# Hymba trunk step: background pieces issued ahead of the newest unit's sigmoids and scans in the prompt attention loop

## The chip, the cores and the metric

The kernel is one program on one core of a Trainium2 chip. The metric is the device time of one execution in microseconds (us). The core's engines each work through a queue of their own, in the order in which the program issued the instructions: PE (TensorE: matmuls, and transposes done as matmuls; PEld is its weight load), DVE (VectorE), ACT (ScalarE), POOL (GpSimd), and SP (SyncE), which here only issues DMAs. PE writes its results to PSUM; DVE and ACT copy them from there.

## The reference, cut to what matters

One layer of a hybrid decoder runs over a prompt (4096 tokens, width 1024) and a sample batch (8 sequences of 4 tokens). Four branches (a state space model, a short convolution, a stick-breaking attention and a cross-attention to 256 memory tokens) read one input projection; each branch is normalized and gated, and an output projection and a last norm follow. The change concerns the prompt's stick-breaking attention, 4 heads of 64 channels:

```python
z = jnp.einsum("nqhd,nkhd->nhqk", q.astype(f32), k.astype(f32)) * (HEAD_DIM ** -0.5)
z = z + bias.astype(f32)[None, :, None, None]
mask = k_pos[None, :] < q_pos[:, None]
log_beta = jax.nn.log_sigmoid(z)
log_1m = jnp.where(mask, jax.nn.log_sigmoid(-z), 0.0)
rev = lax.cumsum(log_1m, axis=3, reverse=True)
excl = jnp.concatenate([rev[..., 1:], jnp.zeros_like(rev[..., :1])], axis=-1)
wts = jnp.where(mask, jnp.exp(log_beta + excl), 0.0)
return jnp.einsum("nhqk,nkhd->nqhd", wts, v.astype(f32)).astype(q.dtype)
```

A weight is sigmoid(z) of its key times the product of sigmoid(-z) over all later keys up to the query. The kernel forms the product as a running product from right to left (a scan on DVE) instead of a sum of logarithms.

## The kernel before, in words

The program has three stretches. Up to about 1970 us it projects the prompt, runs the sample's attention and the other branches. From about 1975 to 3345 us runs the prompt's attention, the subject here. The rest is the tail: the last output tiles.

**Units.** The attention is cut into 72 blocks (query chunk `qc` of 512 tokens, head pair `hp`, key block `kb` of 512 keys from the diagonal back to 0), and each block into four units `qt` of 128 queries: 288 units, numbered 0 to 287. In the text "unit 159" is the 160th; it is also the number of the pass of the loop that begins it. A unit has two heads. On the diagonal (`kb == qc`) it has 128 to 512 keys, elsewhere 512.

**What a pass issues.** The loop at the end of `hymba_kernel` (L1874 to L1898) issues in pass i, in this order:
- `scores` of unit i (L1439): 6 matmuls on PE into two PSUM tiles `z`. There are four such tiles, so the scores of unit i+2 need both heads of unit i to be read to the end.
- in odd passes `out_step` (L1604): one or two pieces of the output projection, 6 matmuls each (L1560 to L1562), which add up to an output tile; DVE adds the residual (`yb<-wo,xt`), and now and then a tile's input is prepared (`mt<-mr`, on ACT and DVE).
- `stage_b` of unit i-3 (L1481): the weights are transposed on PE, head 0 into one PSUM tile `wt`, head 1 into another (L1487), and copied to SBUF (`wT<-wt`), head 1 by ACT, head 0 by DVE, one time in four by ACT. The tag `wt` has two buffers, and almost every matmul of the background writes into the same tag.
- `weights` of unit i (L1456): for each head ACT makes two sigmoids (`om<-z`, `bt<-z`), DVE the scan (L1470, `T<-om,cy,z`; it names `z` as a second operand, so `z` comes free with its end), POOL the product `bt<-bt,T` and a carry `cy` (L1475) for the next key block.
- `run_bg` (L105): each background generator is run to its next `yield`. The sample's generator `smp` is left out before pass 10 and in all odd passes.
- in odd passes `stage_c` (L1493): matmuls of two units' weights with V (`ya<-wT,vt`); at the end of a query chunk's head pair ACT copies and squares `ya`.

**Background generators.** `wout_gen` (L1415): 8 pieces in passes 5 to 12, each loads 128 rows of the output weights and splits them on ACT and DVE (`wo<-stg`). `sample_gen` (L1630): the sample's branches, about a hundred small pieces in even passes to pass 220. `merge_c` (L1520): once for each query chunk, in four pieces: sums of squares on PE (L1525), their copy on ACT (`ev<-so`) and a product with the gate, which is loaded in the same piece (L1531); a matmul (L1535) and `rr` (L1538); nothing; and a transpose (L1544, `bc`) with two products `Yc<-Yc,bc` on DVE. `out_norm` (L1570): for each output tile a square on ACT (`xt<-yb`, with a read of its accumulator), a small DVE step (L1574), a power on POOL, in a following pass a product on DVE (L1577), then the store.

The names at the changed place: `z` in the loop holds the scores of unit i, `sa[i]` its weights, `bg` the list of generators.

Of the kernel before, what the change touches and what calls it, by code (L numbers as in the profile page):

```python
# [29 lines left out]
def hymba_kernel(ctx: ExitStack, tc: tile.TileContext, x_p, x_s, cache_k, cache_v, s_re, s_im, s_conv,  # L30
# [10 lines left out]
    def act(out, in_, f=AF.Copy, **kw):  # L41
        return S.activation(out, in_, f, **kw)  # L42

    def tt(eng, out, a, b, op):
        return eng.tensor_tensor(out=out, in0=a, in1=b, op=op)  # L45
# [59 lines left out]
    def run_bg(skip=None):  # L105
        for g in list(bg):
            if g is not skip and next(g, "end") == "end":
                bg.remove(g)
# [1008 lines left out]
    def load_q(qc, hp):  # L1117
        t = x_tile("qst", F32R).rearrange("p (l n) -> p l n", l=2)
        SP.dma_start(t.bitcast(F32), qscr[:, hp * 128:(hp + 1) * 128, qc * 512:(qc + 1) * 512].rearrange("l p n -> p l n"))
        qst_t[qc, hp] = t  # L1120
# [186 lines left out]
    i = 0  # L1307
# [96 lines left out]
    def load_kv(*b):  # L1404
        load_keys(*b, sb.tile([128, 2, 512], F32R, tag="kst", name="kst", bufs=2))
        load_v2(*b)
# [32 lines left out]
    def scores(qc, hp, kb, qt):  # L1439
        ks = kst_t[qc, hp, kb]  # L1440
        diag = kb == qc
        n = (qt + 1) * 128 if diag else 512

        qs = qst_t[qc, hp]
        zs = [ztile() for h in range(2)]
        for lq_, lk in ((0, 0), (0, 1), (1, 0)):
            for h in range(2):
                r = slice(64 * h, 64 * h + 64)
                mm(zs[h][:, 0:n], qs[r, lq_, qt * 128:(qt + 1) * 128], ks[r, lk, 0:n],  # L1449
                   start=(lq_ + lk == 0), stop=(lq_ == 1 and not diag))  # L1450
        if diag:
            for h in range(2):
                mm(zs[h][:, n - 128:n], idr, maskr, start=False, stop=True)  # L1453
        return zs, n

    def weights(zs, n, qc, hp, kb, qt):  # L1456
        diag = kb == qc
        ws = []
        for h in range(2):
            z, hd = zs[h], 2 * hp + h  # L1460
            om = om2[h]
            T = sb.tile([128, 513], F32, tag="T2", name="T2", bufs=4)
            c = cy[:, 2 * qt + h:2 * qt + h + 1]
            bt = sb.tile([128, 512], F32, tag="bt2", name="bt2", bufs=7)
            act(om[:, 0:n], z[:, 0:n], AF.Sigmoid, scale=-0.125, bias=nb4[:, hd:hd + 1])
            act(bt[:, 0:n], z[:, 0:n], AF.Sigmoid, scale=0.125, bias=b4[:, hd:hd + 1])
            if n < 512:
                V.memset(om[:, n:n + 1], 1.0)

            V.tensor_tensor_scan(T[:, 0:n + 1][:, ::-1], om[:, 0:n + 1][:, ::-1],  # L1470
                                 z[:, 0:1].to_broadcast([128, n + 1]), 1.0 if diag else c,
                                 op0=ALU.mult, op1=ALU.bypass)
            tt(P, bt[:, 0:n], bt[:, 0:n], T[:, 1:n + 1], ALU.mult)
            if kb:
                P.tensor_copy(c, T[:, 0:1])  # L1475
            ws.append(bt)
        return ws, n
# [3 lines left out]
    def stage_b(qt, ws, n):  # L1481

        for h in range(2):
            t = wtp()
            cnt[0] += 1
            for k in range(n // 128):
                tr(t[:, k, :], ws[h][:, k * 128:(k + 1) * 128], ident)  # L1487
            if qt % 2 == 0:
                wts[h] = sb.tile([128, 4, 2, 128], F32, tag="wT2", name="wT2", bufs=4)
            (act if h or cnt[0] % 8 == 1 else V.tensor_copy)(wts[h][:, 0:n // 128, qt % 2, :], t[:, 0:n // 128, :])  # L1490
        return dict(wts)
# [376 lines left out]
    units = [(qc, hp, kb, qt) for (qc, hp, kb) in blocks for qt in range(4)]  # L1868
# [3 lines left out]
    sa, sbq = {}, {}  # L1872
    LAG = 3
    for i in range(nu + LAG + 1):  # L1874
        j = i - LAG
        z = None
        if i < nu:
            qc, hp, kb, qt = units[i]
            if qt == 0:
                bi = i // 4  # L1880
                if bi + 1 < len(blocks):
                    load_kv(*blocks[bi + 1])
                    if blocks[bi + 1][:2] != (qc, hp):
                        load_q(*blocks[bi + 1][:2])
            z = scores(*units[i])
            if i % 2:
                out_step(max(0.0, 8.0 * (4 * NCH - 5) - ost["done"]) * 2 / (nu - i + 1))

        if 0 <= j < nu:
            ws, n = sa.pop(j)  # L1890
            sbq[j] = stage_b(units[j][3], ws, n)
        if z is not None:
            sa[i] = weights(*z, *units[i])
        if i == 5:
            bg.append(wout_gen())
        run_bg(smp if i < 10 or i % 2 else None)
        if j >= 2 and j % 2 == 0:
            stage_c(*units[j - 1], sbq[j - 1])  # L1898
    ost["tail"] = True
# [43 lines left out]
```

## Time and profile before

| | |
|---|---|
| median of 3 runs | 3415.83 us (3399.83 to 3421.22) |
| profiled execution | 3414.53 us, its span 3412.8 us |
| mean granted TensorE clock over the span | 0.973 |
| busy share of the span | PE 93%, PEld 67%, DVE 67%, ACT 52%, POOL 37% |

A row of a group gives busy time, mean time of one instruction, and the idle time of its engine just before it with what ended that idle time. A row of the timeline gives the start, the length from the first start to the last end of what is merged in it, the engine, and in brackets the idle time before it. Waits on several semaphores are put down to the one that came last in the trace.

### The profile page before, as it was taken

How to read it: one execution, taken by the hardware profiler on the slowest of the kernel's cores; microseconds unless marked ns; L12 is line 12 of the kernel's file. 1: busy time of each engine (PE TensorE's matmuls, PEld its weight loads, DVE VectorE, ACT ScalarE, POOL GpSimd, SP SyncE). 2: the span in 40 equal slices, each digit the busy share in tenths (PEclk: the TensorE clock that was granted, in tenths of full speed). 3: DMA queues.
4: the chain of work that ended last, by engine and by line, in shares of the span. 5: the costliest groups of instructions: out<-in, count | busy, mean ns of one | idle time of the engine just before them, and what ended most of it. 6: DMA issues, size and time to landing. Idle time of an engine off the chain costs nothing. (4 is left out here: it accounts for less than half of the span.)

```text
span 3412.8 us, 65273 instructions
## 1 busy us (share of the span) xinstructions
PE 3164.8 (93%) x23383; PEld 2282.1 (67%) x23383; DVE 2283.0 (67%) x3628; ACT 1780.8 (52%) x3324; POOL 1267.6 (37%) x1721
## 2 busy tenths in 40 slices
PE   7888999999999999999999988998999888999998
PEld 6556767667677677676676655666666555666667
DVE  5875667666676676676756566667666777677773
ACT  3435544443444444444434366666656666667771
POOL 1465322222231122222222045555545445555560
PEclk9899999999999999999999979999999999999999
DMA  6677887888877878878887443232323223222223
GB/s 212 194 209 224 279 268 238 264 279 274 267 251 254 286 245 290 263 234 277 270 262 214 142 163 103 91 97 87 97 87 95 71 91 102 94 86 75 88 66 117
DMA packets 382179, 623.57 MB, mean 183 GB/s; under 512 B 54568, under 2 KB 245488, under 8 KB 381856
## 3 DMA queue, kind: packets, MB, share of 16 engines
q1 hardware_dynamic: 344912, 484.90, 45.1%
q0 software_dynamic: 36944, 134.50, 11.9%
q8 instruction: 186, 3.05, 0.4%
q14 instruction: 137, 1.12, 0.1%
HBM read 539.33 MB, written 79.95 MB: 181 GB/s over the span
## 5 line engine op out<-in xcount | busy, mean ns | idle before, releaser
L45 POOL TENSOR_TENSOR bt<-bt,T 128x512 f32<-128x512 f32 (+3 forms) x576 | 605.9, 1052 | 632.2 <-DVE T L1470 417.0
L218 PE MATMUL pj<-xh,whl 128*128 128x512 f32 (+1 forms) x1792 | 724.9, 405 | 0.0
L1470 DVE TENSOR_TENSOR_SCAN T<-om,cy,z 128x513 f32<-128x513 f32 x448 | 549.7, 1268 | 249.3 <-ACT bt L42 96.6
L220 PE MATMUL pj<-xh,whl 128*128 128x512 f32 (+1 forms) x1792 | 658.7, 368 | 9.4 <-DVE whl L45 9.4
L219 PE MATMUL pj<-xh,whl 128*128 128x512 f32 (+1 forms) x1792 | 658.2, 367 | 0.1
L888 POOL DMA_INDIRECT kt<-in_cache_sb_k_dram,idxk x256 | 298.4, 1166 | 898.5 <-DVE kT L1056 787.0
L42 ACT ACTIVATE wT<-wt 128x512 f32<-128x512 f32 (+3 forms) x360 | 194.5, 556 | 448.8 <-PE wt L1487 448.2
L218 PEld LDWEIGHTS pj<-xh,whl 128*128 128x128 f32 x1792 | 344.3, 192 | 120.2 <-issue 82.0
L220 PEld LDWEIGHTS pj<-xh,whl 128*128 128x128 f32 x1792 | 344.0, 192 | 70.3 <-DVE whl L45 12.3
L42 ACT ACTIVATE bt<-z,b 128x512 f32<-128x512 f32 (+3 forms) x576 | 385.2, 669 | 0.0
L42 ACT ACTIVATE om<-z,nb 128x512 f32<-128x512 f32 (+3 forms) x576 | 380.4, 660 | 2.8 <-PE z L1453 2.8
L219 PEld LDWEIGHTS pj<-xh,whl 128*128 128x128 f32 x1792 | 345.6, 193 | 44.9 <-issue 8.6
L1487 PE MATMUL wt<-ident,bt 128*128 128x128 f32 x2112 | 299.5, 281 | 35.2 <-DVE Yc L45 13.5
L1056 DVE STREAM_TRANSPOSE kT<-kt 128x1024 f32<-128x1024 f32 x256 | 315.3, 1232 | 14.9 <-DMA kt<-in_cache_sb_k_dram,idxk 10.3
L1449 PE MATMUL z<-kst,qst 64*128 64x512 f32 (+3 forms) x1704 | 300.1, 424 | 24.2 <-DVE T L1470 21.7
L1487 PEld LDWEIGHTS wt<-ident,bt 128*128 128x128 f32 x2112 | 241.4, 143 | 105.4 <-issue 59.0
L45 DVE TENSOR_TENSOR whl<-stg,whl 128x1024 fp32r<-128x1024 f32 x191 | 234.1, 1226 | 109.3 <-ACT whl L42 99.0
L1503 PE MATMUL ya<-wT,vt 128*64 128x256 f32 (+1 forms) x2176 | 262.8, 382 | 0.3 <-DVE wT L1490 0.3
L42 ACT ACTIVATE whl<-stg 128x1024 fp32r<-128x1024 f32 x192 | 203.1, 1058 | 85.7 <-issue 36.6
L1449 PEld LDWEIGHTS z<-kst,qst 64*128 64x128 f32 x1704 | 152.3, 191 | 129.8 <-issue 52.2
L1560 PE MATMUL wo<-wo,mt 128*128 128x512 f32 x512 | 221.4, 432 | 2.3 <-ACT mt L42 2.3
L1562 PE MATMUL wo<-wo,mt 128*128 128x512 f32 x512 | 206.5, 403 | 0.5 <-DVE mt L45 0.5
(756 smaller groups left out, 4890.5 us busy)
## 6 DMA issues: line engine op xcount, KB each, us to landing
vt<-in_cache_sb_v_dram SPq DMA_DIRECT2D x1024, 128.0 KB
stg<-in_w_in_dram SPq DMA_DIRECT2D x192, 512.0 KB
kst<-kscr SPq DMA_DIRECT2D x71, 512.0 KB
xt<-in_x_prompt_dram SPq DMA_DIRECT2D x64, 512.0 KB
pkt<-pack_d SPq DMA_DIRECT2D x64, 449.0 KB
vt<-vscr SPq DMA_DIRECT2D x71, 256.0 KB
mr<-mscr SPq DMA_DIRECT2D x32, 512.0 KB
out_dram<-yb SPq DMA_DIRECT2D x32, 512.0 KB
```

Source lines behind the costliest of these rows:

```text
L42: return S.activation(out, in_, f, **kw)
L45: return eng.tensor_tensor(out=out, in0=a, in1=b, op=op)
L218: mm(o[:, t0:t1], hi[:, k, :], xh[:, k, 0, t0:t1], start=(k == 0), stop=False)
L219: mm(o[:, t0:t1], hi[:, k, :], xh[:, k, 1, t0:t1], start=False, stop=False)
L220: mm(o[:, t0:t1], lo[:, k, :], xh[:, k, 0, t0:t1], start=False, stop=(k == KT - 1))
L888: P.indirect_dma_start(out=kq[j], out_offset=None, in_=ck_rows, in_offset=bass.IndirectOffsetOnAxis(ap=idxk[:, u // NU, gg:gg + 1], axis=0))
L1056: V.transpose(kts[j], kq.pop(j))
L1449: mm(zs[h][:, 0:n], qs[r, lq_, qt * 128:(qt + 1) * 128], ks[r, lk, 0:n], start=(lq_ + lk == 0), stop=(lq_ == 1 and not diag))
L1470: V.tensor_tensor_scan(T[:, 0:n + 1][:, ::-1], om[:, 0:n + 1][:, ::-1], z[:, 0:1].to_broadcast([128, n + 1]), 1.0 if diag else c, op0=ALU. ...
L1487: tr(t[:, k, :], ws[h][:, k * 128:(k + 1) * 128], ident)
L1503: mm(ya[0][h * 64:h * 64 + 64, q0 * 128:(qt + 1) * 128], v[:, k, h * 64:h * 64 + 64], wTs[h][:, k, q0 - qt + 1:2, :].rearrange("p a b -> p ...
L1560: mm(o, mt[:, k, 0, :], wo[:, k, 0, cs], start=(k == 0), stop=False)
```

## The change

In each pass the call of `weights` moves behind `run_bg`. Nothing else changes: the same instructions, the same buffers.

```diff
         if 0 <= j < nu:
             ws, n = sa.pop(j)
             sbq[j] = stage_b(units[j][3], ws, n)
-        if z is not None:
-            sa[i] = weights(*z, *units[i])
         if i == 5:
             bg.append(wout_gen())
         run_bg(smp if i < 10 or i % 2 else None)
+        if z is not None:
+            sa[i] = weights(*z, *units[i])
         if j >= 2 and j % 2 == 0:
             stage_c(*units[j - 1], sbq[j - 1])
```

`weights` issues nothing on PE and no DMA, so the order on PE and on SP's queue stays as it was; ACT, DVE and POOL change theirs. On DVE, at units 174 to 176, where a chunk's merge ends in an odd pass (the scans stand as SCALAR_TENSOR_TENSOR; `mt` is `out_step`'s, `Yc` the merge's, `g<-wt` the sample's). Before:

```order
L45 TENSOR_TENSOR mt<-mr,mt 128x8x128
L1470 SCALAR_TENSOR_TENSOR T_32698<-om_0_23909,cy,z 128x513
L1470 SCALAR_TENSOR_TENSOR T_32705<-om_1_23910,cy,z 128x513
L45 TENSOR_TENSOR Yc<-Yc,bc 128x512 x2
L1490 COPY wT_32689<-wt 128x4x128
L1470 SCALAR_TENSOR_TENSOR T_32753<-om_0_23909,cy,z 128x513
L1470 SCALAR_TENSOR_TENSOR T_32760<-om_1_23910,cy,z 128x513
L1793 COPY g_32772<-wt 128x512
```

With the change:

```order
L45 TENSOR_TENSOR mt<-mr,mt 128x8x128
L45 TENSOR_TENSOR Yc<-Yc,bc 128x512 x2
L1470 SCALAR_TENSOR_TENSOR T_32707<-om_0_23909,cy,z 128x513
L1470 SCALAR_TENSOR_TENSOR T_32714<-om_1_23910,cy,z 128x513
L1490 COPY wT_32689<-wt 128x4x128
L1793 COPY g_32758<-wt 128x512
L1470 SCALAR_TENSOR_TENSOR T_32760<-om_0_23909,cy,z 128x513
L1470 SCALAR_TENSOR_TENSOR T_32767<-om_1_23910,cy,z 128x513
```

The products `Yc` and the sample's copy `g<-wt`, both of which empty a `wt` buffer, now stand ahead of the scans of their pass instead of behind them.

On ACT, at unit 158, an even pass with an output tile's square. Before:

```order
L42 ACTIVATE wT_31732<-wt 128x4x128
L42 ACTIVATE om_0_23909<-z,nb_88 128x512
L42 ACTIVATE bt_31777<-z,b_87 128x512
L42 ACTIVATE om_1_23910<-z,nb_88 128x512
L42 ACTIVATE bt_31784<-z,b_87 128x512
L42 ACTIVATE xt_30818,ss_31802<-yb 128x1024
```

With the change:

```order
L42 ACTIVATE wT_31732<-wt 128x4x128
L42 ACTIVATE xt_30818,ss_31788<-yb 128x1024
L42 ACTIVATE om_0_23909<-z,nb_88 128x512
L42 ACTIVATE bt_31793<-z,b_87 128x512
L42 ACTIVATE om_1_23910<-z,nb_88 128x512
L42 ACTIVATE bt_31800<-z,b_87 128x512
```

The square of 1024 columns stands ahead of the unit's four sigmoids.

On DVE, at units 158 and 159, the same tile's steps and a sample piece of 158. Before:

```order
L1490 COPY wT_31725<-wt 128x4x128
L1470 SCALAR_TENSOR_TENSOR T_31776<-om_0_23909,cy,z 128x513
L1470 SCALAR_TENSOR_TENSOR T_31783<-om_1_23910,cy,z 128x513
L1801 COPY g_31587<-sms 128x256
L1786 COPY g_31584<-g_31581 64x4 x4
L1574 TENSOR_SCALAR ss_31802<-ss_31802 128x1
L1470 SCALAR_TENSOR_TENSOR T_31846<-om_0_23909,cy,z 128x513
L1470 SCALAR_TENSOR_TENSOR T_31853<-om_1_23910,cy,z 128x513
L1577 SCALAR_TENSOR_TENSOR yb<-yb,ss_31802,fg 128x1024
L1490 COPY wT_31837<-wt 128x4x128
```

With the change:

```order
L1490 COPY wT_31725<-wt 128x4x128
L1801 COPY g_31573<-sms 128x256
L1786 COPY g_31570<-g_31567 64x4 x4
L1574 TENSOR_SCALAR ss_31788<-ss_31788 128x1
L1470 SCALAR_TENSOR_TENSOR T_31792<-om_0_23909,cy,z 128x513
L1470 SCALAR_TENSOR_TENSOR T_31799<-om_1_23910,cy,z 128x513
L1577 SCALAR_TENSOR_TENSOR yb<-yb,ss_31788,fg 128x1024
L1470 SCALAR_TENSOR_TENSOR T_31847<-om_0_23909,cy,z 128x513
L1470 SCALAR_TENSOR_TENSOR T_31854<-om_1_23910,cy,z 128x513
L1490 COPY wT_31837<-wt 128x4x128
```

The sample's copies and L1574 stand ahead of the scans of 158, L1577 ahead of those of 159 and no longer between them and the copy `wT`.

## Rows read from the trace of the kernel before

**Rows 1.** The page's first part, busy time of each engine over the whole span, its share and its instructions.

```profile
PE 3164.8 (93%) x23383; PEld 2282.1 (67%) x23383; DVE 2283.0 (67%) x3628; ACT 1780.8 (52%) x3324; POOL 1267.6 (37%) x1721
```

**Rows 2.** Busy time by stretch (from:to, length, then us and instructions of each engine, granted clock, DMA share, GB/s): the first passes, a stretch of the middle, the last passes of the attention.

```profile
1990.00:2020.00 30.00, 23.62 (x146) 15.39 (x144) 25.49 (x37) 26.55 (x53) 20.70 (x25) 0.78 0.61 195
2400.00:2800.00 400.00, 361.05 (x2366) 251.16 (x2363) 273.66 (x371) 251.34 (x462) 201.05 (x302) 0.96 0.30 91
3200.00:3345.00 145.00, 138.50 (x878) 94.66 (x877) 101.68 (x108) 101.81 (x178) 80.30 (x119) 1.00 0.24 77
```

**Rows 3.** The waits of PE from 1975 to 3345 us: what waited, on what, us in total, times, the longest.

```profile
PE z L1449 <- DVE T L1470: 21.7, 70, 1.2
PE wt L1487 <- DVE Yc L45: 13.5, 7, 3.0
PE wt L1725 <- DVE wT L1490: 7.1, 6, 1.4
...
PE wt L1487 <- DVE g L1793: 4.3, 4, 1.6
PE wt L1487 <- POOL cy L1475: 4.1, 6, 1.4
...
PE wt L1487 <- DVE rr L1538: 3.4, 2, 1.7
...
PE wt L1487 <- DVE g L1711: 1.9, 5, 0.5
...
PE wt L1487 <- DVE g L45: 1.7, 3, 0.6
...
PE wt L1487 <- ACT ev L42: 1.2, 1, 1.2
...
PE wt L1487 <- DVE msT L1661: 1.1, 1, 1.1
```

**Rows 4.** The timeline around the end of a merge, units 174 to 176 (start, length, engine, line, operation).

```profile
2808.40 1.09 POOL L45 TENSOR_TENSOR bt<-bt,T 128x512 f32<-128x512 f32 x1
2808.50 1.02 DVE L1786 COPY g<-g 64x4 f32<-64x4 f32 x1
...
2809.63 0.17 DVE L1786 COPY g<-g 64x4 f32<-64x4 f32 x1
...
2810.38 1.23 DVE L45 TENSOR_TENSOR mt<-mr,mt 128x1024 fp32r<-128x1024 f32 x1
2810.91 0.62 PE L1544 MATMUL bc<-ident,rr 128*128 128x128 f32 x4 [0.34 <-ACT wT L42]
...
2812.49 2.45 DVE L1470 TENSOR_TENSOR_SCAN T<-om,cy,z 128x513 f32<-128x513 f32 x2 [0.89 <-issue]
...
2814.87 1.26 DVE L45 TENSOR_TENSOR Yc<-Yc,bc 128x512 f32<-128x512 f32 x2
...
2816.04 0.68 DVE L1490 COPY wT<-wt 128x512 f32<-128x512 f32 x1
...
2816.27 0.63 PE L1487 MATMUL wt<-ident,bt 128*128 128x128 f32 x4 [1.59 <-DVE Yc L45]
...
2816.78 0.66 PE L1791 MATMUL wt<-ident,g 128*128 128x128 f32 x4
```

**Rows 5.** The timeline around units 158 to 160, with an output tile's square and its product, and two sample pieces.

```profile
2727.19 1.09 ACT L42 ACTIVATE xt<-yb 128x1024 f32<-128x1024 f32 x1
2727.46 1.25 DVE L1470 TENSOR_TENSOR_SCAN T<-om,cy,z 128x513 f32<-128x513 f32 x1
...
2732.74 0.96 PE L1449 MATMUL z<-kst,qst 64*128 64x512 f32 x6
...
2732.86 2.46 DVE L1470 TENSOR_TENSOR_SCAN T<-om,cy,z 128x513 f32<-128x513 f32 x2 [2.16 <-issue]
...
2735.24 1.26 DVE L1577 SCALAR_TENSOR_TENSOR yb<-yb,ss,fg 128x1024 f32<-128x1024 f32 x1
...
2735.41 0.66 PE L1791 MATMUL wt<-ident,g 128*128 128x128 f32 x4 [0.69 <-ACT wT L42]
...
2736.00 0.97 PE L1449 MATMUL z<-kst,qst 64*128 64x512 f32 x6
...
2739.38 0.66 DVE L1793 COPY g<-wt 128x512 f32<-128x512 f32 x1
...
2740.19 0.63 PE L1487 MATMUL wt<-ident,bt 128*128 128x128 f32 x4 [1.20 <-DVE g L1793]
```

**Rows 6.** Busy time by stretch (columns as in Rows 2) of the five stretches in which the clock stood at half right behind one of the waits of Rows 3: the first, the last, and their sum.

```profile
2036.10:2042.90 6.80, 5.87 (x28) 4.40 (x30) 3.06 (x10) 2.75 (x8) 1.92 (x5) 0.50 0.80 222
...
2578.80:2582.20 3.40, 3.40 (x12) 2.27 (x9) 2.16 (x5) 1.50 (x3) 2.58 (x5) 0.50 0.94 311
sum 20.20, PE 19.27 PEld 14.21 DVE 11.39 ACT 12.35 POOL 6.77; mean PE 3.85 PEld 2.84 DVE 2.28 ACT 2.47 POOL 1.35
```

**Rows 7.** Groups of moved work on DVE from 1975 to 3345 us (line, engine, operation, tiles, count, busy us, mean ns of one, idle before).

```profile
L1531 DVE SCALAR_TENSOR_TENSOR Yc<-Yc,gnc,ev 128x512 f32<-128x512 f32 x16 | 11.8, 773 | 4.0 <-DMA ev<-gscr 4.0
L1786 DVE COPY g<-g 64x4 f32<-64x4 f32 x32 | 11.8, 369 | 0.3
...
L45 DVE TENSOR_TENSOR wo<-stg,wo 128x1024 fp32r<-128x1024 f32 x8 | 10.6, 1324 | 0.7 <-ACT wo L42 0.6
```

**Rows 8.** The same for ACT.

```profile
L42 ACT ACTIVATE xt<-yb 128x1024 f32<-128x1024 f32 x26 | 28.2, 1086 | 0.0
...
L42 ACT ACTIVATE wo<-stg 128x1024 fp32r<-128x1024 f32 x8 | 8.7, 1084 | 0.1
L42 ACT ACTIVATION_READ_ACCUMULATOR xt<-yb 128x1 f32 x26 | 5.9, 226 | 0.0
...
L42 ACT ACT_TABLE_LOAD x2 | 2.6, 1283 | 0.0
```

## The prediction, made before the changed kernel was timed

> **What bounds the kernel now.** I read the engine totals first, then the stretches, then PE's waits, then the timeline around two typical places. PE is busy for 93% of the span [rows 1], and in the middle of the attention for 361 of 400 us, against 274 of DVE and 251 of ACT [rows 2]. PE's order stays the same with the change, so the time is PE's work plus PE's idle time, and the question is which idle time goes and which comes. In the middle 39 us of 400 are idle; in the last passes, where the sample's pieces have ended, 6.5 of 145 [rows 2]. The reader should see in the list of waits that PE's idle time has two roots [rows 3]: scores that wait for the scan of two units ago (70 times, 21.7 us, 0.3 us each), and matmuls that wait for one of the two `wt` buffers. Of the latter, those on L1487 wait for a background piece to empty a buffer: 13.5 + 4.3 + 4.1 + 3.4 + 1.9 + 1.7 + 1.2 + 1.1 = 31.2 us (the 4.1 on POOL's `cy` I count with them: after a merge's L1538 that carry was long made). These are the waits that the change is aimed at. Those of background matmuls on the copy `wT`, as L1725's 7.1 us in 6 waits, hang on a copy that stands ahead of both the moved and the unmoved work.
>
> What does delay cost? That differs by the parity of the pass. Unit 158 (even): its second scan ends at 2728.71 and the scores of 160 start at 2732.74, 4.0 us later [rows 5]; in between PE has an output piece to do. Unit 159 (odd): its scans end at 2735.32 and the scores of 161 start at 2736.00, after a wait of 0.69 us in front of a sample matmul [rows 5]. So an even unit's scans can come 2 to 4 us late for nothing, an odd unit's hardly at all. But in the odd pass DVE stood idle 2.16 us before the scans, waiting for ACT's sigmoids [rows 5]: work put there is free.
>
> **The change part by part.**
>
> **End of a merge (odd pass, 8 chunks, 7 waits).** Now `Yc` follows the scans: they end at 2814.94, `Yc` at 2816.13, and the transposes of head 1 wait 1.59 us [rows 4]. With the change `Yc` starts when `mt` and `bc` are done, at about 2811.6, and ends at 2812.9, before those transposes are due at about 2814.6. Before the scans only 0.89 us were free [rows 4], so these start some 0.4 us late, at 2812.9, and end at 2815.4. What is late next: the sample's matmul L1791 waits for the copy `wT`, which follows the scans, to about 2816.1, so here 0.6 of 1.59 us is won; where no sample matmul follows, nearly all. Of 13.5 us I take 10; bounds 0 and 13.5.
>
> **Sample pieces (even pass).** A copy such as L1793 at 2739.38 makes the transposes of the next pass wait 1.20 us [rows 5]. It moves ahead of scans with 2 to 4 us to spare, and behind it PE goes on to `stage_c` and scores that need nothing late. L1793, L1711, `g` on L45, `msT` and `ev` sum to 10.2 us [rows 3]; I take 10, bounds 0 and 10.2.
>
> **The merge's `rr` (odd pass).** 3.4 + 4.1 us [rows 3]. L1538 is small and fits the idle time before the scans, but PE then runs into the same copy `wT` as above in half of the cases. I take 5, bounds 0 and 7.5.
>
> **Clock.** Behind five of these waits the trace shows the clock at 0.50, the 1.2 GHz level, for 20.2 us in all [rows 6], nearly all of it PE work, of which half is lost: 10 us. With the waits mostly gone I take 6; bounds 0 and 10.
>
> **Squares (26 in this stretch, even pass).** 1.09 + 0.23 us on ACT [rows 8] now stand ahead of the four sigmoids. Cover: the 4.0 us of unit 158. Where the following odd pass has one output piece instead of two, the cover is smaller. I take +2; bounds 0 and the whole 34 us (28.2 + 5.9). The sample copies at the same place (as L1786) add about 1 us to DVE, not to ACT, and lie in the same cover. The power on POOL goes ahead of the products; it needs only DVE's small L1574, and nobody waits for it before the next pass.
>
> **L1577 (odd pass).** 1.26 us into 2.16 us of idle time [rows 5]: 0. It no longer stands between the scans and `wT`.
>
> **A merge's first piece (8, even pass).** L1531 waits for a gate tile whose load is issued in the same piece; before, the scans covered that load and the wait was still 4.0 us in all [rows 7]. Now two scans, 2.5 us, no longer cover it, and ACT's `ev` waits for PE ahead of the sigmoids. 2.5 us each, against the cover of 2 to 4: I take +3; bounds 0 and 20.
>
> **The eight `wo` pieces (passes 5 to 12).** Here ACT is busy 26.6 of 30 us and DVE 25.5 [rows 2], and there is no output piece to make cover. 1.08 us on ACT each, then 1.32 on DVE [rows 7, 8], the second beside the first sigmoid. In a stretch that ACT fills the order matters little: +3; bounds 0 and 8.7.
>
> **The sample's softmax piece (once).** It loads a table, 1.28 us [rows 8], waits for DVE, and loads back; ahead of the sigmoids that is about 5 us against 3 of cover: +2.
>
> **Buffers.** `wt` hands out its two buffers otherwise in about ten places: seven background matmuls now wait for DVE's copy instead of ACT's, three the reverse. By 7.1 / 6 = 1.2 us [rows 3] against 0.69 [rows 5] that is 4 x 0.5: +2; bounds -2 and +5.
>
> **Pairs of DVE and POOL.** The first of four small copies L1786 takes 1.02 us, a later one 0.17, and it ends when POOL's product ends (2808.40 + 1.09) [rows 4]. So moved pieces may meet a product at their new place too. On odd passes POOL is idle there, on even ones DVE's `wT` uses up 0.68 of the 1.09 us: 0 in the sum, as it lies in the cover. The Trainium skill (SBUF — State Buffer, section "SBUF: two separate sides") says that DVE and GpSimd share one pair of ports as an exclusive lock for a whole instruction, whoever comes first, for DVE operations with two SBUF inputs too; by that rule the eight `wo` steps, each behind a product of the unit before, could lose up to a whole product each. That is rival D.
>
> **Sum.** -10 -10 -5 -6 = -31, and +2 +3 +3 +2 +2 = +12: -19 us. Against the profiled execution of 3414.5 us this gives **3395 us**. The median of the runs, 3415.8, differs by 1.3 us and changes nothing.
>
> **The rivals.**
> - **A, the wait is handed on.** The freed transposes are followed at once by scores or a sample matmul that hang on the odd scans, as at unit 175, where 0.6 of 1.59 us remain. If all places were like it, 25 becomes about 10, the clock gives nothing, and with +12 the time is about 3416. For: 70 waits of scores on scans already. Against: most sample pieces sit in even passes. It is also what happens if the freed buffer is not the one awaited.
> - **B, more falls away.** The whole 31 us, 10 from the clock, and half of the costs: 3414.5 - 41 + 6, about 3380, and lower if sample matmuls wait less for a `wT` that is no longer behind L1577. For: the covers of 2 to 4 us. Against: the loop through the odd unit is nearly closed.
> - **C, slower.** The covers are not there: a piece at the head of ACT or DVE holds up the sigmoids and scans behind it, in even passes as well. Price: squares 34.1, L1786 11.8, L1531 11.8 [rows 7, 8], together +58; with the freed waits at 16 that gives about 3456. It decides from the point where an even unit's scans end after the scores two units on are due, 4.0 us at unit 158 [rows 5]. Speaks against it: delays of 1.3 to 2.5 us are below that.
> - **D, the port.** Up to 1.1 us on each of eight `wo` steps in a stretch without cover: +9, 3404.
>
> **How the numbers follow.** The forecast (3383 to 3408) has 0.52, A 0.14, B 0.18, C 0.09, D 0.07. About 1%, 34 us, is what a measurement of this kernel can tell from no change: faster means below 3382, slower above 3450. Faster: most of B and a little of the forecast's edge, 0.23. Slower: most of C, 0.08. Within 1%: 0.69. The range reaches from B's middle with somewhat more, 3368, to A with its costs doubled, 3428; outside lie C and B's end.
>
> **What would show it.** In the trace after: PE's waits on `Yc`, `g` and `rr` gone from L1487's row (step right if 31 us fall below 8); scores' waits on scans, 21.7 us, growing by no more than 10 (if by 20, A); DVE's idle time before the scans filled, by L1577 in odd passes; the scores of an even unit + 2 still starting after its scans (if PE waits there, C); the first 30 us of the `wo` pieces no longer than 33; the granted clock at or above 0.973. I am wrong if the time comes out above 3428 with the L1487 waits gone, for then a cover that I read at one unit does not hold for the others.

## The result, and the profile after

| | before | after |
|---|---|---|
| median of 5 runs each, side by side | 3407.11 us (3399.83 to 3421.22) | 3381.80 us (3378.01 to 3391.03) |
| ratio after to before, 95% interval | | 0.9917 [0.9897, 0.9937] |
| profiled execution | 3414.53 us | 3391.03 us |
| span and mean granted clock | 3412.8 us, 0.973 | 3389.3 us, 0.974 |

The change gains 0.83%, some 28 us (21 to 35). The profiled executions differ by 23.5 us. All of it lies in the prompt's attention. At first the changed kernel falls behind: unit 4 begins 1.2 us later than before, unit 13, after the `wo` pieces, 3.5 us later. From there it gains: unit 18 begins 0.1 us earlier, unit 96 15 us, unit 240 24 us.

The totals of the page after, to be held against [rows 1]: the same instructions, PE a little shorter.

```profile
PE 3156.3 (93%) x23383; PEld 2280.9 (67%) x23383; DVE 2278.2 (67%) x3628; ACT 1780.1 (53%) x3324; POOL 1252.3 (37%) x1721
```

Busy time by stretch after (columns as in [rows 2]): passes 5 to 12, from the scores of unit 5 to those of unit 13, the middle, and the whole attention.

```profile
1986.18:2019.26 33.08, 27.18 (x159) 18.05 (x158) 24.18 (x43) 26.41 (x57) 16.32 (x26) 0.76 0.61 193
...
2400.00:2800.00 400.00, 364.39 (x2371) 255.88 (x2370) 271.63 (x381) 249.90 (x460) 198.15 (x300) 0.95 0.30 90
...
1975.00:3322.00 1347.00, 1232.30 (x7963) 851.25 (x7964) 958.24 (x1254) 902.99 (x1661) 708.52 (x1063) 0.97 0.31 96
```

The first and the last of these for the kernel before:

```profile
1984.95:2015.74 30.79, 25.62 (x159) 17.34 (x158) 24.28 (x42) 26.54 (x56) 19.11 (x24) 0.78 0.61 196
...
1975.00:3345.00 1370.00, 1237.07 (x7952) 849.23 (x7952) 961.39 (x1253) 902.16 (x1658) 723.02 (x1063) 0.96 0.30 94
```

PE's idle time in the attention is the length minus the busy time: 1370.00 - 1237.07 = 132.9 us before, 1347.00 - 1232.30 = 114.7 us after. So 18 us of the 23 are idle time; the rest is PE work that took 4.8 us less, because less of it ran at 1.2 GHz: the clock record of these two stretches has 102.0 us at 0.50 before and 92.2 after, and half of the difference is 4.9.

The waits of PE after (to be held against [rows 3]):

```profile
PE z L1449 <- DVE T L1470: 29.5, 77, 1.5
PE wt L1725 <- DVE wT L1490: 9.7, 8, 1.4
PE wt L1791 <- DVE wT L1490: 9.2, 8, 1.4
...
PE so L1525 <- DVE smr L1650: 2.1, 1, 2.1
...
PE wt L1487 <- DVE rr L1538: 0.9, 1, 0.9
PE wt L1487 <- DVE ss L1574: 0.8, 1, 0.8
PE wt L1487 <- ACT wT L42: 0.8, 1, 0.8
PE wt L1487 <- ACT ev L42: 0.7, 1, 0.7
```

`Yc`, `g` and the carry are gone from L1487's waits, and 0.9 us of `rr` is left. But two other kinds grew: scores on scans from 21.7 to 29.5 us, and background matmuls on `wT`, as L1725 from 7.1 to 9.7.

### The profile page after: what moved, and what is told of

The parts are those of the page before. It is cut to its first block, busy times and chain, and to the rows that moved or that the text cites. A ratio compares the mean times of both kernels' runs of the same rounds, so it can differ in the third digit from the quotient of the medians.

```text
span 3389.3 us, 65303 instructions
## 1 busy us (share of the span) xinstructions
PE 3156.3 (93%) x23383; PEld 2280.9 (67%) x23383; DVE 2278.2 (67%) x3628; ACT 1780.1 (53%) x3324; POOL 1252.3 (37%) x1721
## 3 DMA queue, kind: packets, MB, share of 16 engines
q0 software_dynamic: 36944, 134.50, 12.1%
## 5 line engine op out<-in xcount | busy, mean ns | idle before, releaser
L1449 PE MATMUL z<-kst,qst 64*128 64x512 f32 (+3 forms) x1704 | 302.1, 423 | 32.6 <-DVE T L1470 29.5
L1487 PE MATMUL wt<-ident,bt 128*128 128x128 f32 x2112 | 292.7, 280 | 3.3 <-DVE rr L1538 0.9
L1487 PEld LDWEIGHTS wt<-ident,bt 128*128 128x128 f32 x2112 | 242.5, 143 | 65.7 <-issue 40.8
```

## Where the time went: the accounts of all runs

A table by run. For each I summed PE's idle time between the first and the last transpose of L1487 by what the waiting matmul was (scores, L1487, everything else = background), and the time at 0.50 in the trace's clock record, from the entries that begin and end in that stretch (the one that runs across its start adds 8 to 12 us in every row). One profiled execution each, so a difference of 2 or 3 us, or of 10 us at half clock, is not to be read; even the first transpose of L1487, ahead of which the versions hardly differ, came anywhere from 1973.1 to 1983.0 us. The stretch begins and ends a little inside the one above, so the sums are slightly smaller. The ratio is that of the runs, with its 95% interval; us are (ratio - 1) x 3410.

The columns "full clock" and "clock" split the gain by the runs themselves, for each has its span and mean granted clock on record. Span times clock is the span that would be left if nothing were lost at 1.2 GHz, an estimate that takes PE to be at work there throughout ([rows 6]: 19.27 of 20.20 us); span times (1 - clock) is what the clock took. Given is the mean against the runs of the kernel before beside it, with a 95% interval (for the change, against 70 runs of the kernel before from the experiments). In these 70 the first part is 3322 to 3326 us in each of four groups and scatters by 2 to 3 us from run to run, the second is 82 to 89 us and scatters by 4 to 7: executions of one kernel differ mostly by clock.

| pieces ahead of the scans | ratio | us | full clock | clock | idle | L1487 | scores | background | at 1.2 GHz |
|---|---|---|---|---|---|---|---|---|---|
| none (before) | 1 | 0 | 0 | 0 | 132.0 | 35.2 | 24.2 | 72.6 | 85.3 |
| all (the change) | 0.9917 [0.9897, 0.9937] | -28 | -18 ±5 | -9 ±10 | 113.6 | 3.3 | 32.6 | 77.7 | 78.5 |
| in odd passes only | 0.9964 [0.9952, 0.9976] | -12 | -12 ±2 | -1 ±5 | 119.0 | 8.3 | 27.9 | 82.7 | 75.1 |
| in even passes only | 0.9924 [0.9904, 0.9945] | -26 | -14 ±3 | -10 ±8 | 121.2 | 22.5 | 29.5 | 69.2 | 75.1 |
| output norm only | 1.0008 [0.9994, 1.0022] | +3 | -2 ±2 | +4 ±5 | 130.6 | 30.9 | 24.3 | 75.4 | 105.8 |
| all but the output norm | 0.9877 [0.9859, 0.9894] | -42 | -27 ±8 | -12 ±9 | 109.2 | 3.9 | 29.9 | 75.5 | 71.7 |
| all but the squares' piece | 0.9962 [0.9944, 0.9980] | -13 | -18 ±2 | +4 ±6 | 117.1 | 4.3 | 33.0 | 79.8 | 78.5 |
| all but L1577 | 0.9889 [0.9868, 0.9910] | -38 | -30 ±5 | -11 ±8 | 108.0 | 3.9 | 29.1 | 75.0 | 58.0 |
| odd passes, no output norm | 0.9963 [0.9948, 0.9978] | -13 | -13 ±3 | 0 ±7 | 121.1 | 13.8 | 27.4 | 79.9 | 92.2 |
| even passes, no output norm | 0.9952 [0.9939, 0.9964] | -16 | -14 ±3 | -4 ±8 | 119.9 | 22.1 | 28.6 | 69.3 | 54.6 |
| all, ACT pad in even passes | 0.9999 [0.9984, 1.0013] | 0 | -9 ±2 | +8 ±6 | 118.6 | 1.7 | 40.7 | 76.2 | 88.7 |
| all, ACT pad in odd passes | 1.0207 [1.0180, 1.0235] | +71 | +40 ±3 | +27 ±16 | 161.1 | 2.9 | 79.2 | 79.0 | 119.5 |
| all but the output norm, `wT` copies exchanged | 0.9719 [0.9705, 0.9734] | -96 | -75 ±3 | -22 ±6 | 58.5 | 3.3 | 24.6 | 30.7 | 44.4 |
| none, `wT` copies exchanged | 0.9775 [0.9761, 0.9789] | -77 | -55 ±3 | -22 ±4 | 78.5 | 29.2 | 20.1 | 29.2 | 37.5 |

The first two rows give the change's books: 31.9 us of L1487's waits fell away, 8.4 came back in front of scores and 5.1 in front of background matmuls. So 42% was handed on and 18.4 us of idle time was won, which is what the runs gain at full clock (18, give or take 5). The other 9 or so of the 28 us are the clock's, and these the runs don't tell from nothing (give or take 10).

## The experiments

**Which passes gain?** The call of `weights` stays in its old place in passes of one parity.

```diff
+        if z is not None and i % 2 == 0:
+            sa[i] = weights(*z, *units[i])
         if i == 5:
...
-        if z is not None:
+        if z is not None and not (i % 2 == 0):
             sa[i] = weights(*z, *units[i])
```

So the pieces are ahead in odd passes only; the second run has `i % 2 == 1` in both places.

> The background runs ahead of the newest unit's sigmoids and scans in odd passes alone. Theory 1 (the gain is PE's waits for a wt buffer that a background piece empties): the waits on Yc (13.5 us) and rr (3.4 + 4.1) go, those on g (4.3 + 1.9 + 1.7) stay; with a third handed on to the copy wT, 10 to 16 us less than the kernel before. Theory 2 (the gain is L1577 no longer standing between the odd scans and the copy wT): nearly the whole gain of the full change, 24 us or more, since L1577 sits in odd passes.

> The background runs ahead in even passes alone. Theory 1: the waits on g, msT and ev (10.2 us) go, those on Yc and rr stay; the squares, the merge's first pieces and the softmax piece cost 0 to 7 us; 4 to 12 us less than before. Theory 2: no gain, or up to 10 us more than before, for only costs are left.

Both gain: the odd part the 10 to 16 us of Theory 1, the even part 26 where that theory had 4 to 12. Theory 2, no gain without L1577's move, is out. The odd part frees most of L1487's waits (35.2 to 8.3), the even part fewer (to 22.5), and yet their idle time falls about alike, by 13.0 and 10.8 us, because the even part hands less on: background waits fall by 3 us there and rise by 10 in the odd part. At full clock the runs gain about alike too, 12 and 14 us. What is left of the even part's lead is clock, and no run shows where it comes from. The reader should keep this: how much of a named wait vanishes says little; the sum of the idle time says more, and the clock is to be booked beside it.

**What does the output norm do?** Its generator alone is moved, or all the others without it: `run_bg` is called twice, ahead of `weights` and behind it, with a choice by the generator's name (the choice inside `run_bg` is left out here; the first run has `==` for `!=`).

```diff
-        run_bg(smp if i < 10 or i % 2 else None)
+        ahead = lambda n: n != 'out_norm'
+        run_bg(smp if i < 10 or i % 2 else None, ahead)
         if z is not None:
             sa[i] = weights(*z, *units[i])
+        run_bg(smp if i < 10 or i % 2 else None, lambda n: not ahead(n))
```

> Only the output norm's pieces (square, L1574, power, L1577, store) run ahead of the sigmoids and scans, all others behind them as before. Theory 1: no wt buffer is emptied earlier, so the time is that of before within 5 us; the L1487 waits stay above 25 us. Theory 2: 15 to 25 us less than before.

> All pieces but the output norm's run ahead. Theory 1: the whole gain of the change, 22 to 30 us less than before, perhaps 2 more for the squares that no longer stand ahead of the sigmoids. Theory 2: at most 8 us less than before.

Moved alone it changes nothing that can be measured. Among the others it takes back 14 us: 0.9877 against 0.9917, a difference of 0.0040 with an interval of about 0.0027 to either side, so 14 us, give or take 9 (9, give or take 8, at full clock). The version without it is the first that beats the change, and by more than the 22 to 30 us expected of it.

**Which half of the output norm?** The same two calls, with `ahead = lambda n: n != 'out_norm' or i % 2 == 1` (L1577 ahead, squares behind) and with `== 0` (squares ahead, L1577 behind).

> All background pieces ahead of the newest unit's scans, but of the output norm only its odd-pass piece (L1577 ahead of the odd scans); its even-pass piece (squares, POOL's power and product) stays behind, as before. With all pieces ahead -28 us, with all but the output norm -42, so 14 us are to be placed. Theory P (L1577 at its new place meets POOL's product, which the square pushed late; both moves are needed): about -40, L1577 at 1.26 to 1.28 us mean, waits of scores behind L1577 about 4.5 us in all. Theory Q (the square's 1.3 us of ACT ahead of the even sigmoids cost by themselves): about -40 too. Theory R (L1577 ahead of the odd scans costs by itself): about -28, waits of scores in these odd passes near 9 us.

> The mirror of the kernel before it: of the output norm only the even-pass piece (squares on ACT, power and product on POOL) is ahead of the scans, L1577 of the odd pass stays behind them, all other background pieces are ahead. Theory P (meeting of L1577 and POOL's product): about -40, L1577 near 1.27 us, since behind the scans the product is long done. Theory Q (the squares cost by themselves): about -28. Theory R (L1577's place costs): about -40.

With the squares ahead and L1577 behind, -38 us: nothing of the 42 that can be measured is lost. That is what R expected, and P too; Q is out. With L1577 ahead and the squares behind, only -13, far off P's and Q's -40 and less even than R's -28. The groups show why this run is no clean half. L1577 of that run:

```profile
L1577 DVE SCALAR_TENSOR_TENSOR yb<-yb,ss,fg x33: 1272/1283/1287, 2101.8 to 3387.7; 128x1024 f32<-128x1024 f32 x32, 32x1024 f32<-32x1024 f32 x1
its engine sat idle before it (us, times) until:
  POOL ss L45: 32.6, 23
```

Its consumer is ahead, its producer is not: L1577 at the head of DVE's queue waits for POOL's power `ss`, 1.4 us each of 23 times (32.6 / 23), and the odd scans wait behind it. It is never stretched here (at most 1.287 us). Scores wait 10.4 us in the passes with an output tile, against 4.5 without the output norm ahead, and PE's idle time is 7.9 us larger (117.1 against 109.2). At full clock the run lies 9 us behind that version (18 against 27), give or take 9; the rest of the 29 us between them is clock. In the changed kernel itself `ss` is there in time, and L1577 is stretched instead:

```profile
L1577 DVE SCALAR_TENSOR_TENSOR yb<-yb,ss,fg x33: 1248/1275/1955, 2099.9 to 3384.3; 128x1024 f32<-128x1024 f32 x32, 32x1024 f32<-32x1024 f32 x1
```

The timeline of the changed kernel around unit 149 (start, length, engine, line, operation) shows one of the eight places at which it took 1.8 us or more:

```profile
2666.89 1.09 POOL L45 TENSOR_TENSOR bt<-bt,T 128x512 f32<-128x512 f32 x1
...
2667.11 1.95 DVE L1577 SCALAR_TENSOR_TENSOR yb<-yb,ss,fg 128x1024 f32<-128x1024 f32 x1
...
2667.93 1.18 POOL L1475 COPY cy<-T 128x1 f32<-128x1 f32 x1
...
2668.99 2.44 DVE L1470 TENSOR_TENSOR_SCAN T<-om,cy,z 128x513 f32<-128x513 f32 x2
...
2670.31 0.50 PE L1449 MATMUL z<-kst,qst 64*128 64x512 f32 x1 [1.52 <-DVE T L1470]
...
2671.48 0.95 PE L1449 MATMUL z<-kst,qst 64*128 64x512 f32 x5 [0.68 <-DVE T L1470]
```

POOL's product of unit 148 began at 2666.89 and ended at 2667.98. L1577 began 0.22 us after it and ended at 2669.06, 1.08 us after the product's end (1.07 or 1.08 us at all eight places, which began 0.22 to 0.36 us after a product). The odd scans, which follow it, start at 2668.99, and the scores wait 1.52 + 0.68 us. Where L1577 stands behind the scans, as in the run "all but L1577", the same place reads:

```profile
2655.30 2.46 DVE L1470 TENSOR_TENSOR_SCAN T<-om,cy,z 128x513 f32<-128x513 f32 x2 [0.88 <-POOL bt L45]
...
2656.64 0.50 PE L1449 MATMUL z<-kst,qst 64*128 64x512 f32 x1 [0.40 <-DVE T L1470]
...
2657.68 1.26 DVE L1577 SCALAR_TENSOR_TENSOR yb<-yb,ss,fg 128x1024 f32<-128x1024 f32 x1
```

The scores' first wait is 0.40 us instead of 1.52. A wait like that has a second price. Stretches of the changed kernel (columns as before): the 8.8 us up to the end of these waits, and what came then.

```profile
2664.00:2672.80 8.80, 6.61 (x42) 4.52 (x41) 8.51 (x8) 7.16 (x13) 5.79 (x8) 1.00 0.34 119
2672.80:2676.20 3.40, 3.40 (x13) 2.80 (x12) 3.33 (x5) 0.37 (x1) 1.16 (x2) 0.50 0.57 159
```

PE was busy 6.61 of 8.80 us, and then the granted clock stood at 0.50, the 1.2 GHz level, for 3.4 us of pure work, 1.7 us lost. The same follows unit 189, at 2870.8. With L1577 behind, unit 189 has no such stretch, unit 149 still one after its 0.40 and 0.68 us. So with L1577 behind, PE is idle 5.6 us less (113.6 - 108.0), and 1.7 us of slow clock fall away: 7 of the 10 to 14 us. Of the rest of the 20 us at half clock by which the two profiled executions differ, 3.4 lie before the first L1577 and some 14 at other places behind it; what they hang on stays open.

What follows: R is right in its core where all other pieces are ahead too. There L1577 costs 10 us at full clock, give or take 6 (the change against "all but L1577", with 5.6 us of idle time in the traces), and what the traces show of it is odd scans that come late. It isn't so everywhere: with the output norm alone ahead L1577 was stretched at seven places, with the odd pieces alone ahead it waited 23.4 us for `ss`, and neither version is slower for it by anything that can be measured (+3 us against the kernel before; -12 against -13 without it, below). Their scores waited 5.2 and 6.7 us in these passes, where the change has 9.1 and the kernel before 4.5. How much of it is the stretch and how much the 1.26 us that L1577 takes anyway isn't separated: of the 9.1 us of scores' waits in the passes with an output tile, 6.8 fall into the eight stretched ones, but there L1577 also began latest. A kernel in which L1577 stands ahead and meets no product wasn't tried.

**How much cover is there?** The changed kernel with two useless copies on ACT right ahead of the sigmoids, in even or in odd passes (the tile `pad` is left out).

```diff
+            if i % 2 == 0:
+                for _ in range(2):
+                    act(pad, fg[:, 0:320])
             sa[i] = weights(*z, *units[i])
```

> The changed kernel with two useless ACT copies of 320 columns (about 0.8 us together, an estimate) ahead of the sigmoids of every even pass (144 passes). Theory of the cover (an even unit's scans can come 2 to 4 us late for nothing): 0 to +8 us against the changed kernel, so -28 to -20 against the kernel before; waits of scores on scans near 33 us as without the copies. Rival (both parities alike, or ACT close to being the bound): +50 or more, up to 144 x 0.8 = 115.

> The same two copies ahead of the sigmoids of every odd pass instead. Theory of the cover (an odd unit's scans can hardly be late): most of 144 x 0.8 us, +50 to +110 against the changed kernel, so +20 to +80 against the kernel before, with the waits of scores on scans grown by as much. Rival (parities alike): the same as for the even passes.

The pad's own group, then its place in the timeline of the odd run:

```profile
L42 ACT ACTIVATE pad<-fg x288: 452/469/543, 1977.4 to 3382.9; 128x320 f32<-128x320 f32 x144
...
2703.09 0.97 ACT L42 ACTIVATE pad<-fg 128x320 f32<-128x320 f32 x2
2703.97 0.67 ACT L42 ACTIVATE om<-z,nb 128x512 f32<-128x512 f32 x1
```

A pair puts the sigmoids off by 2703.97 - 2703.09 = 0.88 us, 127 us in 144 passes. Against the changed kernel the odd pads cost 0.0290 x 3410 = 99 us, and PE's waits for odd scans tell it at once:

```profile
PE z L1449 <- DVE T L1470: 78.0, 143, 1.6
```

The even pads cost 0.0082 x 3410 = 28 us (16 by the profiled spans, 3405.1 against 3389.3). So the parities do differ, by 3.5 to 5 times; but the cover of the even passes isn't free, where I had expected 0 to 8 us: an eighth to a fifth of the delay is paid. Much of that is clock: at full clock the even pads cost 9 us and the odd ones 58, in idle time 5.0 and 47.5.

**Do the parities add up?** The two parity runs again, without the output norm: `ahead = lambda n: n != 'out_norm' and i % 2 == 1`, and `== 0`.

> Background pieces ahead of the scans in odd passes only, and the output norm's pieces behind everywhere. With L1577 among the odd pieces it was -12 us, with L1577 and the even pieces but the squares -13, with all but the output norm -42. Theory S (L1577, whose ss came late because the squares stayed behind, took back some 27 us in both of those runs; most of the gain is the odd merge pieces): about -35 to -40, waits on L1487 near 8 us. Theory T (the parities add up: odd -15, even -27): about -15. The prediction's own sum for the odd part (Yc and rr, with their share of the clock) is -15 to -19.

> Background pieces ahead of the scans in even passes only, without the output norm's. With the squares ahead as well it was -26 us, waits on L1487 22.5 us. Theory S (odd and even pieces overlap in what they cure): about -20 to -28, since the squares cost nothing in their cover. Theory T (they add up to -42): about -27. If the squares' 1.3 us of ACT in each of 26 passes cost something, about -40. The prediction's own sum for the even part without squares is near 0: -10 for the sample's copies and +8 to +10 of costs.

Theory S falls for the odd part: without L1577 the odd part is still only -13, so in odd-only it was not L1577 that hid a large gain. T holds there. The even part, -16 (12 to 21), is smaller than any of its three readings had it. In idle time the two are simply additive: -10.9 and -12.1 against -22.8 for both. In us they are not quite: -13 and -16 against -42 leaves 13, give or take 9, which the idle time doesn't account for. It lies in the clock: at full clock the runs give -13 and -14 against -27 (give or take 3, 3 and 8). The squares ahead cost nothing: 0.9924 with them, 0.9952 without, with intervals that meet.

**What is left?** In the kernel after as before, PE's largest idle time is that of background matmuls which wait for a `wT` copy on DVE. So I let the two copies change engines: head 0's, whose buffer comes free first and is wanted first, to ACT, and head 1's to DVE.

```diff
-            (act if h or cnt[0] % 8 == 1 else V.tensor_copy)(wts[h][:, 0:n // 128, qt % 2, :], t[:, 0:n // 128, :])
+            (V.tensor_copy if h and cnt[0] % 8 != 2 else act)(wts[h][:, 0:n // 128, qt % 2, :], t[:, 0:n // 128, :])
```

> All pieces ahead but the output norm (-42 us), and the two copies of stage_b (wT<-wt on L1490) change engines: head 0 on ACT and head 1 on DVE, with the same one in eight turned over to the other engine. What is left of PE's idle time is led by background matmuls that wait for a wT copy on DVE, some 55 us in all against 15 for those on ACT. If DVE's copy is late because it stands behind scans, the swap hands these matmuls ACT's copy instead and wins up to 20 us more: -45 to -62. Rival: ACT's copy then stands between the sigmoids and is late as well, or DVE's copy of head 1 pushes the odd scans: 0 to +40 against the version without the swap.

> The kernel before, in its own order of pieces, with the two wT copies exchanged alone (head 0 on ACT, head 1 on DVE). Together with the moved pieces the exchange was worth about 55 us on top of 42. If the two are independent (the copy wT that comes first in the round is what background matmuls hang on, whatever stands ahead of the scans): -45 to -60, background matmuls' waits fallen from some 73 us to 30, L1487's waits near 30 as before. If the exchange only pays because the moved pieces empty the other buffer in time (otherwise the wait moves to L1487): 0 to -25, with L1487's waits above 40 us.

-96 us with the moved pieces (all but the output norm), -77 us without any: the exchange alone is worth nearly three times the change. An output tile's odd pass around unit 159 in the changed kernel:

```profile
2719.35 2.46 DVE L1470 TENSOR_TENSOR_SCAN T<-om,cy,z 128x513 f32<-128x513 f32 x2 [1.78 <-ACT bt L42]
...
2721.30 0.60 ACT L42 ACTIVATE wT<-wt 128x512 f32<-128x512 f32 x1 [0.83 <-PE wt L1487]
...
2721.72 0.67 DVE L1490 COPY wT<-wt 128x512 f32<-128x512 f32 x1
...
2721.95 1.09 POOL L45 TENSOR_TENSOR bt<-bt,T 128x512 f32<-128x512 f32 x1
...
2722.45 0.66 PE L1791 MATMUL wt<-ident,g 128*128 128x128 f32 x4 [1.18 <-DVE wT L1490]
```

DVE's copy stands behind two scans that end at 2721.81; the matmul that wants its buffer waits 1.18 us, while ACT, which was idle for 0.83 us, copies the buffer that is wanted later. With the copies exchanged (and the pieces moved):

```profile
2667.16 0.60 ACT L42 ACTIVATE wT<-wt 128x512 f32<-128x512 f32 x1 [0.39 <-PE wt L1487]
...
2667.81 0.66 PE L1791 MATMUL wt<-ident,g 128*128 128x128 f32 x4 [0.25 <-ACT wT L42]
```

The matmul waits 0.25 us. The middle stretch and the first of the waits of that run:

```profile
2400.00:2800.00 400.00, 386.25 (x2593) 269.31 (x2589) 298.45 (x418) 277.82 (x502) 219.66 (x332) 0.98 0.31 97
```

```profile
PE z L1449 <- DVE T L1470: 21.1, 52, 0.9
```

13.75 of 400 us idle, where it was 35.61 after the change and 38.95 before. The moved pieces are worth 0.0056 x 3410 = 19 us, give or take 7, on top of the exchange, not 42; in the run with the exchange alone L1487 still waits, but partly on something else:

```profile
PE wt L1487 <- ACT wT L42: 11.2, 15, 0.9
...
PE wt L1487 <- DVE Yc L45: 1.9, 1, 1.9
```

Of the 13.5 us on `Yc` 1.9 are left there, though no piece was moved; why, I didn't follow up. My expectation for it, -45 to -60, was too small, as was that for both together.

## Why the prediction was right, and where it was not

The forecast was 3395 us in a range of 3368 to 3428, and the time was 3381.8: inside, 0.83% below the kernel before, so within 1%, though right at the 3382 named as its edge. By its own sum it is -19 us against a measured -28 [-35, -21], so the sum is some 2 to 16 us too small. Of the 13 us between 3395 and 3381.8, some 7 have nothing to do with the mechanism: the forecast starts from the profiled execution, 3414.5, and the five runs of the kernel before have their median at 3407.1. In the sum's own terms the profiled executions give -31.9 + 5.1 = -27 for L1487's waits with the buffers (forecast -25 + 2), +8.4 in front of scores (forecast +10 for squares, merges, `wo` and softmax, and 0 for L1577), and -3 to -5 for the clock (forecast -6). So the totals were right, and one part of the +8.4 came from where nothing was forecast. Point by point:

- **L1487's waits.** "step right if 31 us fall below 8": 3.3 us are left. Right. The gains of 25 from them are near the truth as well: at the end of a merge `Yc` now starts ahead of the scans (after, around unit 175), and the sample's matmul behind it waits 0.74 us where the transposes waited 1.59 [rows 4]; 0.85 won, 0.6 forecast:

```profile
2795.62 1.28 DVE L45 TENSOR_TENSOR Yc<-Yc,bc 128x512 f32<-128x512 f32 x2 [2.02 <-PE bc L1544]
...
2796.82 2.45 DVE L1470 TENSOR_TENSOR_SCAN T<-om,cy,z 128x513 f32<-128x513 f32 x2
...
2799.19 0.67 DVE L1490 COPY wT<-wt 128x512 f32<-128x512 f32 x1
...
2799.91 0.66 PE L1791 MATMUL wt<-ident,g 128*128 128x128 f32 x4 [0.74 <-DVE wT L1490]
```

- **Scores on scans**, "growing by no more than 10": 21.7 to 29.5, 7.8 more. Right. Rival A did happen, but to a smaller share: it was to hand on 15 of 25, and 13.5 of 31.9 came back; its time, 3416, is out.
- **The squares.** +2 forecast; waits of scores on even scans grew from 0.4 to 2.9 us in all, but of the places with a square only unit 188 has one (0.98 us, and the softmax piece stands there too); the runs with the squares ahead are no slower than those without. So the cover held. A timeline of the changed kernel around units 158 and 159, ACT, DVE and the scores of unit 160:

```profile
2711.47 1.05 ACT L42 ACTIVATE xt<-yb 128x1024 f32<-128x1024 f32 x1
...
2713.95 2.45 DVE L1470 TENSOR_TENSOR_SCAN T<-om,cy,z 128x513 f32<-128x513 f32 x2
2716.31 1.26 DVE L1577 SCALAR_TENSOR_TENSOR yb<-yb,ss,fg 128x1024 f32<-128x1024 f32 x1
...
2719.29 0.96 PE L1449 MATMUL z<-kst,qst 64*128 64x512 f32 x6
2719.35 2.46 DVE L1470 TENSOR_TENSOR_SCAN T<-om,cy,z 128x513 f32<-128x513 f32 x2 [1.78 <-ACT bt L42]
```

  The even scans end at 2716.40 and the scores of unit 160 start at 2719.29: 2.9 us of cover left of 4.0 [rows 5].
- **L1577, "1.26 us into 2.16 us of idle time: 0".** This is the step that failed. At unit 159 it is true (1.78 us of idle time are left above). Elsewhere it isn't: mean 1.437 us up to 3345 us against the 1.26 of [rows 5], 1.8 us and more in eight places, and the scores' waits in the passes of an output tile 9.1 us against 4.5. With the other pieces ahead, moving it cost some 10 us, give or take 6, where 0 was forecast. The reason given, "on odd passes POOL is idle there", was read at one unit; at the eight others POOL's product still ran when L1577 began. That it is late because the square ahead of the sigmoids makes the even unit's scans late follows from the order of the queues; no run shows that link by itself.
- **Pairs of DVE and POOL, rival D.** The port was put at the wrong place. The `wo` steps got no longer, 1242 ns against 1324 [rows 7], and the small copies L1786 even shorter, since they now stand where no product runs. The groups after, to be held against [rows 7]:

```profile
L1577 DVE SCALAR_TENSOR_TENSOR yb<-yb,ss,fg 128x1024 f32<-128x1024 f32 (+1 forms) x29 | 41.7, 1437 | 0.5 <-POOL ss L45 0.5
L1531 DVE SCALAR_TENSOR_TENSOR Yc<-Yc,gnc,ev 128x512 f32<-128x512 f32 x16 | 11.7, 748 | 12.1 <-DMA ev<-gscr 12.1
L45 DVE TENSOR_TENSOR wo<-stg,wo 128x1024 fp32r<-128x1024 f32 x8 | 9.9, 1242 | 8.9 <-ACT wo L42 8.9
...
L1786 DVE COPY g<-g 64x4 f32<-64x4 f32 x32 | 5.2, 162 | 0.3
```

- **A merge's first piece**, +3. The wait came as named, L1531's for its load grew from 4.0 to 12.1 us, but at none of the merges do the scores two units on wait for scans. It costs nothing that shows: too high by 3.
- **The `wo` pieces**, +3. DVE's wait ahead of `wo` grew from 0.7 to 8.9 us, and passes 5 to 12 took 33.08 us instead of 30.79: 2.3 us more, at the edge of the 33 named. The sum had this about right.
- **The softmax piece**, +2: the scores of unit 190 wait 0.98 us for scans, but the sample's matmul L1812 behind them waits 0.69 us instead of 2.12. It costs nothing that shows. The wait `so` on `smr`, 2.1 us, is another sample piece's, and at that place `so` waited 3.0 us for `wT` before.
- **Buffers**, +2 with -2 to +5: background waits grew by 5.1 us, the upper bound. That 5.1 includes L1791 and L1725, whose `wT` now follows L1577 or `Yc`, a cost that the prediction booked only for the merges.
- **Clock**, -6: in the profiled executions 6.8 us less at half speed, 9.8 with the entry across the start, so -3 to -5; by the runs -9, give or take 10. That doesn't tell -6 from its neighbours. The L1487 waits no longer lead to it, but one in front of L1725 (1.4 us, and 1.2 GHz from 2454.3) and those for late odd scans do.
- **Rival B** (about 3380) is nearest in time, and one of its grounds was met: the whole 31 us fell away. The others were not: 13.5 us came back where 12 of costs were forecast, so they were not halved, L1577 cost more than forecast, and what it hoped for from `wT` went the other way. That its number fits is luck of the base: it is a gain of 35 us from 3414.5, and 28 from 3407 were measured.
- **Rival C** put its point at delays of 4 us in even passes. The pads show that delay there does cost before that, an eighth to a fifth of it, clock included; in odd passes two thirds and more. Its price, 58 us of work that all reaches the end, was far off.

## What to carry to other kernels

When work moves ahead of the instructions that close a loop, sort it by what it hangs on in the queue: work that empties a buffer (here the copies from `wt`) belongs ahead, long work for which nobody waits soon behind (L1577 ahead cost some 10 us once all else was ahead, and nothing measurable by itself). Keep a consumer behind its own producer: L1577 ahead without its squares waited 1.4 us for `ss` at 23 places. The cover must be read at several places, those among them where the neighbouring engine has been made late by the same change. And before the order of the background is tuned, look at which engine empties the buffer that is wanted first: giving that copy to the engine with idle time was worth 77 us alone, the reordering 28.

## What the runs showed of the hardware

POOL and DVE held each other up in both directions, and only for some operations. L1577 (two inputs in SBUF) took 1.95 us instead of 1.26 when it began 0.22 us after a product on POOL; POOL's carry, a copy of one column that takes 0.18 us alone, took 1.18 us when it was issued beside L1577, and ended at 2669.11 with it (2669.06). The small copy L1786 took 1.02 us beside a product and 0.17 without [rows 4]. The scans, of which 251 of the 480 at full width run beside a product for over 0.6 us, were never stretched:

```profile
L1470 DVE TENSOR_TENSOR_SCAN T<-om,cy,z x448: 1150/1259/1284, 2024.6 to 3304.5; 128x513 f32<-128x513 f32 x150
```

(this row is of the changed kernel; minimum, median and maximum in ns). Nor were DVE's copies out of PSUM: 0.67 us beside a product, as at 2721.72 above, where one ran at 2721.95. The Trainium skill (SBUF — State Buffer, section "SBUF: two separate sides") says that the pair of ports which the two engines share is an exclusive lock for a whole instruction, taken by a DVE operation with two SBUF inputs against a GpSimd one that reads SBUF. The traces here agree: L1577 was blocked, the scan, whose second array `z` lies in PSUM, was not. The prediction applied this rule to the `wo` steps, which were not stretched; it showed at L1577.
